# The first two rows of query weights multiplied with the two token tiles one by one

## The chip, the cores and the metric

The kernel runs on one core of one Trainium2 chip. The metric is the device time of one execution in microseconds (us). TensorE is called PE here, its weight loads PEld, VectorE DVE, ScalarE ACT, GpSimd POOL; SP issues DMAs.

## The reference

The program is an encoder trunk of two layers over 256 tokens of width 1024. Each layer has a mixer (retention, a linear recurrence and attention side by side, with one input and one output projection) and then a PEER channel mixer. The PEER part, cut to what matters here:

```python
def peer(x, wq, keys, u, v):          # x: the tokens after RMSNorm
    q = (xt @ wq).reshape(T, PEER_HEADS, 2, PEER_HALF)     # 256 x 1024 @ 1024 x 2048
    s = jnp.einsum('thpk,hpnk->thpn', q, keys, ...)
    sv, si = lax.top_k(s, PEER_TOPK)
    ...
    # gather 16 experts per head and token, gelu, weighted sum
```

## The kernel before

Tokens are held transposed: `hT` and `lT` are 128 x 8 x 256, that is eight blocks `d` of 128 channels by 256 tokens. `hT` is the value rounded to the matmul's 4-byte format, `lT` the rest that the rounding took away. Each weight tile is split the same way into `hi` (ACT, line 140) and `lo` (DVE or POOL, line 141). A product is then made of three matmuls (`three`, lines 205 to 207): hi with hT, hi with lT, lo with hT. The weights are the stationary operand, 128 x 128, and the tokens are the moving operand, 256 columns at a time. Every matmul has a weight load of its own ahead of it.

The tokens come as two tiles of 128 rows. At the end of the mixer the output projection (`wout`) is done for token tile 0, then `norm_T` normalises that tile, transposes it on PE (line 197), and writes its 128 columns of `hT` (ACT, line 201) and `lT` (DVE, line 202). The same follows for tile 1. While DVE, POOL and ACT normalise tile 1, PE has no more output projection to do.

`peer` begins with the query projection. Its loop runs over four blocks `b` of 512 query columns, and in each over four weight tiles `d2`; one weight tile has two rows `k` of 128 channels and four groups `c` of 128 columns, so 2 x 4 x 3 = 24 matmuls of 256 columns. The results gather in two PSUM banks `pq`. After the last `d2`, ACT copies them out (line 719), and PE makes the scores with the keys (line 723). The four raw tiles and four hi/lo pairs are rotating buffers. Splits of block 0 go to DVE for even `d2` and to POOL for odd ones.

A scheduler, not the order of the code alone, sets the order in which each engine gets its instructions; within an engine they run in that order, and one that waits holds up all behind it.

Of the kernel before, what the change touches and what calls it, by code (L numbers as in the profile page):

```python
# [18 lines left out]
P = 128  # L19
D = 1024  # L20
T = 256
NT = 2
DEPTH = 2
EPS = 1e-6
ND = D // P
# [84 lines left out]
def trunk(ctx, tc, x, rows, lru_col, lru_gw, w_in, w_out, ln2_w, peer_wq, peer_kt, peer_ut, peer_v, lnf_w,  # L110
# [9 lines left out]
    def acc_tile():  # L120
        return ps.tile([P, 512], F32, tag="acc", bufs=4, name="acc")
# [4 lines left out]
    def hd_tile():  # L126
        return ps.tile([P, 512], F32, tag="hd", bufs=2, name="hd")

    def raw_tile():
        return sp.tile([P, D], F32, tag="raw", bufs=RAW, name="raw")  # L130

    def hl_tiles():
        return (sp.tile([P, D], F32R, tag="hi", bufs=HL, name="hi"),
                sp.tile([P, D], F32R, tag="lo", bufs=HL, name="lo"))

    def eng(pattern, a):
        return G if pattern[a % len(pattern)] == "G" else V

    def split(src, hi, lo, lo_eng=None):
        A.activation(hi, src, AF.Copy)  # L140
        (lo_eng or V).tensor_sub(lo, src, hi.bitcast(F32))  # L141
# [62 lines left out]
    def three(o, lh, ll, rh, rl, first, last, skip=False):  # L204
        TE.matmul(o, lh, rh, start=first, stop=False, skip_group_check=skip)  # L205
        TE.matmul(o, lh, rl, start=False, stop=False, skip_group_check=skip)  # L206
        TE.matmul(o, ll, rh, start=False, stop=last, skip_group_check=skip)  # L207

    hT = cp.tile([P, ND, T], F32R, name="hT")
    lT = cp.tile([P, ND, T], F32R, name="lT")  # L210
# [389 lines left out]
    def peer(l, pp):  # L600
# [100 lines left out]
        for b in range(4):  # L701
            pq = [acc_tile() for _ in range(2)]
            for d2 in range(4):
                raw = raw_tile()
                nc.sync.dma_start(raw.rearrange("p (k c) -> p k c", k=2),
                                  peer_wq[l, d2 * 2 * P:(d2 + 1) * 2 * P, b * 512:(b + 1) * 512]
                                  .rearrange("(k p) c -> p k c", p=P))
                hi, lo = hl_tiles()
                split(raw, hi, lo, eng(WP0 if b == 0 else WP1, d2))
                for k in range(2):  # L710
                    d = d2 * 2 + k
                    for c in range(4):
                        s = slice(k * 512 + c * P, k * 512 + (c + 1) * P)
                        o = pq[c // 2][:, (c % 2) * T:(c % 2 + 1) * T]
                        first, last = d == 0 and c % 2 == 0, d == ND - 1
                        three(o, hi[:, s], lo[:, s], hT[:, d], lT[:, d], first, last, skip=True)
                sa.adv(2.4)
            for c in range(2):
                A.activation(qs[:, 2 * c:2 * c + 2], pq[c].rearrange("p (k t) -> p k t", k=2), AF.Copy)
            for tt in (1, 0):  # L720
                pt = hd_tile()
                for k in range(4):
                    TE.matmul(pt[:, k * NK:(k + 1) * NK], qs[:, k, tt * P:(tt + 1) * P], keyT[:, b * 4 + k],
                              start=k == 0, stop=True, skip_group_check=True)
                A.activation(scs[:, tt, b * 4:b * 4 + 4], pt.rearrange("p (k n) -> p k n", k=4), AF.Copy)  # L725
            sa.add(topk(1, b))
# [146 lines left out]
    for l in range(layers):  # L873
        with tc.tile_pool(name=f"mp{l}", bufs=1) as mp, tc.tile_pool(name=f"ms{l}", bufs=2) as ms:
            mix(l, mp, ms)
        if do_peer:
            with tc.tile_pool(name=f"pp{l}", bufs=1) as pp:
                peer(l, pp)
# [50 lines left out]
```

## Time and profile before

| | us |
|---|---|
| median of 3 runs | 1975.18 (1974.17 to 1978.27) |
| the profiled execution | 1973.99 |
| its span, first to last instruction | 1972.2 |
| PE busy in it | 1881.7 (95%) |
| mean granted PE clock | 0.979 |

A row of a timeline gives the start in us from the span's start, the duration, engine, line, operation, output and inputs, and how many instructions were merged in the row; in brackets stands the idle time of the engine before it and what ended that. Durations of pipelined matmuls overlap, so the pace of a run of them is read from the distance between starts. Of the two levels of the PE clock, 1.2 and 2.4 GHz, a granted clock of 0.50 is the lower and 1.00 the upper.

### The profile page before, as it was taken

What the parts mean: (1) busy time and instruction counts of PE and PEld (TensorE: products, weight loads), DVE (VectorE), ACT (ScalarE), POOL (GpSimd) and SP (SyncE); (2) the same over time, 40 slices, a digit from 0 to 9 for tenths busy, and PEclk for the clock granted to TensorE, in tenths of its full rate; (3) what the DMA queues carried; (4) which work ended last, traced back from release to release, by engine and by line L of the source; (5) the groups of instructions that cost most, each with busy time, mean ns of one, the idle gap of its engine ahead of it and who ended that gap; (6) DMA issues with size and microseconds to landing.
All of it is one profiled execution on the core that took longest, in us unless ns stands there. A gap on an engine that the chain in (4) does not pass through costs nothing. (4 is left out here: it accounts for less than half of the span.)

```text
span 1972.2 us, 34047 instructions
## 1 busy us (share of the span) xinstructions
PE 1881.7 (95%) x13348; PEld 1662.5 (84%) x13348; DVE 1512.7 (77%) x2716; ACT 901.0 (46%) x1378; POOL 563.3 (29%) x238
## 2 busy tenths in 40 slices
PE   6888999999999999999978889999999999999998
PEld 5658999999999877788866689999999998777886
DVE  6965999789855699755569569995997557996555
ACT  4444544444444443444454344445434444434443
POOL 3615788200000134100056168881000002440000
PEclk9988999999999999999988899999999999999999
DMA  5405555545555544555454055555445555446553
GB/s 185 145 25 182 162 190 183 192 154 163 166 183 192 171 139 161 185 189 191 151 164 132 23 198 170 184 185 191 151 160 172 189 186 171 150 142 201 185 189 128
DMA packets 95280, 324.41 MB, mean 164 GB/s; under 512 B 10128, under 2 KB 10640, under 8 KB 94864
## 3 DMA queue, kind: packets, MB, share of 16 engines
q1 hardware_dynamic: 92384, 314.61, 49.0%
q10 hardware_dynamic: 2736, 7.63, 1.1%
q8 instruction: 104, 1.70, 0.3%
q14 instruction: 56, 0.46, 0.1%
HBM read 321.16 MB, written 1.05 MB: 163 GB/s over the span
## 5 line engine op out<-in xcount | busy, mean ns | idle before, releaser
L140 ACT ACTIVATE hi<-raw 128x1024 fp32r<-128x1024 f32 (+1 forms) x600 | 627.3, 1047 | 529.2 <-issue 176.9
L141 POOL TENSOR_TENSOR lo<-raw,hi 128x1024 fp32r<-128x1024 f32 (+1 forms) x202 | 530.4, 2633 | 919.8 <-ACT hi L140 900.1
L141 DVE TENSOR_TENSOR lo<-raw,hi 128x1024 fp32r<-128x1024 f32 x398 | 491.6, 1236 | 201.9 <-ACT hi L140 201.9
L205 PE MATMUL acc<-hi,ph 128*128 128x512 f32 x1024 | 410.2, 401 | 0.0
L207 PE MATMUL acc<-hi,pl 128*128 128x512 f32 x1024 | 404.8, 396 | 0.4 <-DVE pl L141 0.4
L206 PE MATMUL acc<-lo,ph 128*128 128x512 f32 x1024 | 404.9, 395 | 0.0
L205 PE MATMUL tr<-hT,hi 128*128 128x256 f32 x1024 | 290.8, 284 | 0.0
L205 PE MATMUL hd<-hT,hi 128*128 128x256 f32 x1024 | 290.5, 284 | 0.0
L140 ACT ACTIVATE ph<-Gt 128x256 fp32r<-128x256 f32 x256 | 106.4, 417 | 400.6 <-PE acc L206 389.6
L206 PE MATMUL hd<-lT,hi 128*128 128x256 f32 x1024 | 287.8, 281 | 0.0
L206 PE MATMUL tr<-lT,hi 128*128 128x256 f32 x1024 | 287.6, 281 | 0.0
L207 PE MATMUL hd<-hT,lo 128*128 128x256 f32 x1024 | 287.5, 281 | 0.0
L207 PE MATMUL tr<-hT,lo 128*128 128x256 f32 x1024 | 287.5, 281 | 0.0
L207 PEld LDWEIGHTS acc<-hi,pl 128*128 128x128 f32 x1024 | 192.4, 188 | 48.2 <-DVE pl L141 2.4
L206 PEld LDWEIGHTS acc<-lo,ph 128*128 128x128 f32 x1024 | 192.9, 188 | 41.4
L205 PEld LDWEIGHTS acc<-hi,ph 128*128 128x128 f32 x1024 | 192.7, 188 | 41.3 <-ACT ph L140 0.5
L141 DVE TENSOR_TENSOR pl<-Gt,ph 128x256 fp32r<-128x256 f32 x256 | 124.6, 489 | 127.7 <-ACT ph L140 127.7
L205 PEld LDWEIGHTS hd<-hT,hi 128*128 128x128 f32 x1024 | 193.1, 189 | 1.5 <-ACT Gt L725 0.4
L205 PEld LDWEIGHTS tr<-hT,hi 128*128 128x128 f32 x1024 | 193.1, 189 | 1.1
L206 PEld LDWEIGHTS tr<-lT,hi 128*128 128x128 f32 x1024 | 193.0, 188 | 1.0
L206 PEld LDWEIGHTS hd<-lT,hi 128*128 128x128 f32 x1024 | 193.0, 188 | 0.9
L207 PEld LDWEIGHTS hd<-hT,lo 128*128 128x128 f32 x1024 | 192.9, 188 | 0.0
(204 smaller groups left out, 2622.6 us busy)
## 6 DMA issues: line engine op xcount, KB each, us to landing
raw<-in_peer_ut_dram SPq DMA_DIRECT2D x256, 512.0 KB, 3.4
raw<-in_peer_v_dram SPq DMA_DIRECT2D x256, 512.0 KB, 4.2
raw<-in_peer_wq_dram SPq DMA_DIRECT2D x32, 512.0 KB, 3.8
raw<-in_w_in_dram SPq DMA_DIRECT2D x24, 512.0 KB, 3.6
raw<-in_w_out_dram SPq DMA_DIRECT2D x16, 512.0 KB, 3.4
raw<-in_w_in_dram SPq DMA_DIRECT2D x16, 384.0 KB, 3.4
Gt<-in_peer_kt_dram ACTq DMA_DIRECT2D x2, 1024.0 KB, 6.1
row<-in_rows_dram ACTq DMA_DIRECT2D x4, 256.0 KB, 4.9
```

Source lines behind the costliest of these rows:

```text
L140: A.activation(hi, src, AF.Copy)
L141: (lo_eng or V).tensor_sub(lo, src, hi.bitcast(F32))
L205: TE.matmul(o, lh, rh, start=first, stop=False, skip_group_check=skip)
L206: TE.matmul(o, lh, rl, start=False, stop=False, skip_group_check=skip)
L207: TE.matmul(o, ll, rh, start=False, stop=last, skip_group_check=skip)
```

## The change

For the first weight tile of the first block (`b == 0 and d2 == 0`) the 24 matmuls of 256 columns become two passes of 24 matmuls of 128 columns: first token tile 0, then token tile 1. Everything else keeps its code. In both layers this makes 48 matmuls, each with its weight load, out of 24.

```diff
-                for k in range(2):
-                    d = d2 * 2 + k
-                    for c in range(4):
-                        s = slice(k * 512 + c * P, k * 512 + (c + 1) * P)
-                        o = pq[c // 2][:, (c % 2) * T:(c % 2 + 1) * T]
-                        first, last = d == 0 and c % 2 == 0, d == ND - 1
-                        three(o, hi[:, s], lo[:, s], hT[:, d], lT[:, d], first, last, skip=True)
+
+                parts = [slice(tt * P, (tt + 1) * P) for tt in range(NT)] if b == 0 and d2 == 0 else [slice(0, T)]
+                for t in parts:
+                    for k in range(2):
+                        d = d2 * 2 + k
+                        for c in range(4):
+                            s = slice(k * 512 + c * P, k * 512 + (c + 1) * P)
+                            o = pq[c // 2][:, (c % 2) * T + t.start:(c % 2) * T + t.stop]
+                            first, last = d == 0 and c % 2 == 0 and t.start == 0, d == ND - 1
+                            three(o, hi[:, s], lo[:, s], hT[:, d, t], lT[:, d, t], first, last, skip=True)
```

The order of the instructions on DVE, ACT, POOL and SP is the same in both programs. On PE it differs at two places, one in each layer. The first is in layer 0, PE's queue at the end of the output projection; `tr` is the PSUM tile of the transposes of token tile 1, `hi_1250` and `lo_1251` are the first query weight tile, `acc_1246` and `acc_1247` the two banks `pq`. Before:

```order
L197 MATMUL tr_1221<-ident_71,raw_1208 128x128 [waits DVE_49,PE_49]
L197 MATMUL tr_1221<-ident_71,raw_1208 128x128 x3
L197 MATMUL tr_1229<-ident_71,raw_1208 128x128 [waits DVE_49,PE_49]
L197 MATMUL tr_1229<-ident_71,raw_1208 128x128 x3
L205 MATMUL acc_1246<-hT_75,hi_1250 128x256 [waits Activation_49]
L205 MATMUL acc_1247<-hT_75,hi_1250 128x256
L206 MATMUL acc_1246<-lT_76,hi_1250 128x256 [waits DVE_49]
L207 MATMUL acc_1246<-hT_75,lo_1251 128x256
```

And the same place now:

```order
L205 MATMUL acc_1246<-hT_75,hi_1250 128x128 [waits Activation_49]
L197 MATMUL tr_1221<-ident_71,raw_1208 128x128 [waits DVE_49,PE_49]
L197 MATMUL tr_1221<-ident_71,raw_1208 128x128 x3
L197 MATMUL tr_1229<-ident_71,raw_1208 128x128 [waits DVE_49,PE_49]
L197 MATMUL tr_1229<-ident_71,raw_1208 128x128 x3
L206 MATMUL acc_1246<-lT_76,hi_1250 128x128
L207 MATMUL acc_1246<-hT_75,lo_1251 128x128 [waits DVE_49]
L205 MATMUL acc_1246<-hT_75,hi_1250 128x128
```

One matmul of token tile 0 stands ahead of the transposes of tile 1; the other 47 stand behind them, and the first wait on DVE after the transposes is now on `lo` (line 141) and not on `lT` (line 202).

The passage from token tile 0 to tile 1, PE in layer 0, now:

```order
L205 MATMUL acc_1247<-hT_75,hi_1250 128x128
L206 MATMUL acc_1247<-lT_76,hi_1250 128x128
L207 MATMUL acc_1247<-hT_75,lo_1251 128x128
L205 MATMUL acc_1246<-hT_75,hi_1250 128x128 [waits Activation_49]
L206 MATMUL acc_1246<-lT_76,hi_1250 128x128 [waits DVE_49]
```

The waits for tile 1's `hT` and `lT` have moved here, 24 matmuls further back. In layer 1 PE's queue differs in the same way, one matmul ahead of the eight transposes and 47 behind them.

## Rows read from the trace of the kernel before

**Rows 1.** The page, first part: busy us, share and instructions of each engine.
```profile
PE 1881.7 (95%) x13348; PEld 1662.5 (84%) x13348; DVE 1512.7 (77%) x2716; ACT 901.0 (46%) x1378; POOL 563.3 (29%) x238
```
**Rows 2.** Timeline of PE, layer 0, end of output projection and first query weights.
```profile
157.21 0.39 PE L207 MATMUL acc<-hi,mixL 128*128 128x512 f32 x1
161.53 1.94 PE L197 MATMUL tr<-ident,raw 128*128 128x128 f32 x8 [3.93 <-DVE raw L188]
163.30 0.79 PE L205 MATMUL acc<-hT,hi 128*128 128x256 f32 x2
165.73 0.58 PE L206 MATMUL acc<-lT,hi 128*128 128x256 f32 x1 [1.63 <-DVE lT L202]
166.11 0.41 PE L207 MATMUL acc<-hT,lo 128*128 128x256 f32 x1
...
169.95 0.32 PE L205 MATMUL acc<-hT,hi 128*128 128x256 f32 x1
170.11 0.28 PE L206 MATMUL acc<-lT,hi 128*128 128x256 f32 x1
...
170.35 0.28 PE L205 MATMUL acc<-hT,hi 128*128 128x256 f32 x1
```
**Rows 3.** Timelines of DVE and ACT, same stretch, and DVE's next row behind it.
```profile
161.69 3.38 DVE L141 TENSOR_TENSOR lo<-raw,hi 128x1024 fp32r<-128x1024 f32 x1
165.00 1.27 DVE L202 TENSOR_TENSOR lT<-tr,hT 128x512 fp32r<-128x512 f32 x2
...
181.99 0.30 DVE L635 MAX8 Gt<-Gt 128x8 f32<-128x128 f32 x1 [14.58 <-ACT Gt L725]
...
159.51 1.99 ACT L140 ACTIVATE hi<-raw 128x1024 fp32r<-128x1024 f32 x2
```
**Rows 4.** Timeline of PE, the same place in layer 1.
```profile
1138.44 1.06 PE L197 MATMUL tr<-ident,raw 128*128 128x128 f32 x8 [3.93 <-DVE raw L188]
...
1142.63 0.58 PE L206 MATMUL acc<-lT,hi 128*128 128x256 f32 x1 [2.09 <-DVE lT L202]
1143.01 0.41 PE L207 MATMUL acc<-hT,lo 128*128 128x256 f32 x1
...
1146.00 0.39 PE L207 MATMUL acc<-hT,lo 128*128 128x256 f32 x1
...
1146.94 0.28 PE L205 MATMUL acc<-hT,hi 128*128 128x256 f32 x1
```
**Rows 5.** Timelines of DVE and ACT in layer 1.
```profile
1138.61 3.37 DVE L141 TENSOR_TENSOR lo<-raw,hi 128x1024 fp32r<-128x1024 f32 x1
...
1136.42 1.99 ACT L140 ACTIVATE hi<-raw 128x1024 fp32r<-128x1024 f32 x2
```
**Rows 6.** Weight loads of lines 478 and 207: duration ns min/median/max, first and last start.
```profile
L478 PEld LDWEIGHTS hd<-pT,vt x64: 132/136/231, 119.6 to 1107.1; 128*64 128x64 f32 x64
L207 PEld LDWEIGHTS acc<-hT,lo x320: 186/188/333, 16.8 to 1195.5; 128*128 128x128 f32 x160
```
**Rows 7.** Timeline of PE, the scores of block 0, and the line's instruction count.
```profile
179.01 1.16 PE L723 MATMUL hd<-Gt 128*128 128x128 f32 x8
179.92 0.37 PE L205 MATMUL acc<-hT,hi 128*128 128x256 f32 x1
...
L723 PE MATMUL hd<-Gt x128: 270/275/377, 179.0 to 1198.4; 128*128 128x128 f32 x128
```
**Rows 8.** Busy us by engine, PE clock granted, DMA share and GB/s, by stretch.
```profile
166.00:170.00 4.00, 4.00 (x20) 4.00 (x21) 1.41 (x2) 0.39 (x1) 0.00 (x0) 0.50 0.86 254
170.00:174.00 4.00, 4.00 (x35) 4.00 (x35) 0.00 (x0) 2.42 (x3) 3.25 (x2) 1.00 0.72 277
...
112.00:116.00 4.00, 4.00 (x12) 2.41 (x11) 2.62 (x9) 2.28 (x8) 0.00 (x0) 0.50 0.00 0
...
200.00:210.00 10.00, 9.96 (x85) 9.76 (x84) 9.93 (x36) 5.34 (x7) 8.05 (x4) 1.00 0.51 158
```
**Rows 9.** Timeline of PE in the stretch of layer 0 from 111.5.
```profile
111.54 3.66 PE L446 MATMUL hd<-kT,qT 64*128 64x256 f32 x8 [0.85 <-ACT pr L457]
```

## The prediction

> **What bounds the kernel now.** I read the page first: PE is recorded busy for 95% of the span [rows 1], so a change on PE counts wherever the others keep up. Then I read PE's timeline where the change sits. After the last matmul of the output projection at 157.21 PE waits 3.93 us for DVE to normalise token tile 1, transposes it from 161.53, runs two query matmuls at 163.30, and waits again, 1.63 us, until DVE has written `lT` [rows 2]. From 165.73 on it runs without a gap. DVE's own timeline says why `lT` is late: the 3.38 us `lo` of the first weight tile stands ahead of it and ends at 161.69 + 3.38 = 165.07; the first half of `lT` follows [rows 3]. Layer 1 is the same: 3.93 us, then 2.09 us until 1142.63, with `lo` ending at 1138.61 + 3.37 = 1141.98 [rows 4, 5]. The idle time is what the change could fill. Behind this place PE has no slack (9.96 of 10 us busy in a later stretch [rows 8]), and DVE's next instruction waits 14.58 us for scores that PE makes [rows 3]. So a shift of PE here goes to the end in full.
>
> **What the order allows.** Only one of the 48 matmuls stands ahead of the transposes. It needs the first of two ACT splits, done near 159.51 + 1.0 = 160.5 in layer 0 and 1137.4 in layer 1 [rows 3, 5], and so it falls into the idle time before 161.53 and 1138.44: cost nothing, covered by 1.0 us. If the split came later than that, the transposes, `hT` and `lT` queued behind it would be late by as much. Behind the transposes one more matmul has its data; the next waits for `lo`. The 3.93 us wait is therefore not filled at all. What is won is that PE goes on when `lo` is ready and not half an `lT` later: 165.73 - 165.12 = 0.61 us in layer 0 and 1142.63 - 1142.03 = 0.60 in layer 1 (0.05 us allowed from the end of `lo` to PE). Tile 1's `hT` and `lT`, now needed 22 matmuls later, are long done then. No DMA moves; the orders of DVE, ACT, POOL and SP are unchanged, and a later PE only gives the weight tiles more time.
>
> **What 128 columns cost.** No matmul of 128 columns in this format is in the trace, so I bound it. The pace at 256 columns is 0.213 us at 1.2 GHz (166.11 to 169.95 in 18 steps) and 0.118 at 2.4 GHz [rows 2]. If only the moving columns counted, half of that would do: 0.107 and about 0.06. But each matmul loads 128 columns of 4-byte weights. The loads of 64 such columns take 132 to 136 ns and those of 128 take 186 to 188; at the lower clock the maxima are 231 and 333 [rows 6]. So 64 columns more cost 52 ns at the upper and 102 ns at the lower level, and 128 columns stream for 104 to 108 ns and about 205 to 213: as long as the 256 moving columns do. Loads cannot be quicker than that one after another, so I take the old pace for the new matmul: 0.213 us low, and high the 0.113 us at which 128-column f32 passes with such loads follow each other ((179.92 - 179.01) / 8) [rows 7]. The split then halves no time and doubles the count.
>
> The Trainium skill ("TensorE: Matmul & The Clock Gate", LDWEIGHTS) puts a weight load at its columns divided by 1.2, in ns, whatever the clock: 107 ns for 128. The trace agrees at the upper level and not at the lower, where loads take longer [rows 6]; by that rule the lower-level pace would be 0.107 and the change would come out as the second rival below. The same page (Back-to-back issue gap) gives about 81 ns for load and matmul pairs of 128 columns at full clock; no row here shows that, and by it the first rival would come to about 1978.
>
> **The sum if the clock stays low.** In layer 0 the third matmul starts at 165.12; the restart took 0.38 us before [rows 2], so the fourth starts at 165.50, and the 49th (the first of the next weight tile) 45 x 0.2133 = 9.60 us later, at 175.10. Before, that tile began with the 25th at 170.35 [rows 2]: 4.75 us lost. In layer 1: 1142.03 + 0.38 + 9.60 = 1152.01 against 1146.94 [rows 4]: 5.07 us lost. Together 9.8.
>
> Does the clock stay low? Before, it rose 4.2 us (169.95) and 3.5 us (1146.1) after PE began to run without gaps [rows 2, 4, 8]. Recorded busyness is not what raises it: from 112 to 116 PE shows 4.00 of 4 us busy at a granted 0.50 [rows 8], in matmuls that use 64 of the 128 rows [rows 9]. A stretch in which the array waits half of its time for weights looks to me more like that one than like the dense one, so I expect 1.2 GHz through the whole split. Then the clock comes back some time within the next tile. Between no delay and the 4.2 us seen before, 0 to 20 matmuls run at 0.213 instead of 0.118: 0 to 1.9 us a layer; I take 1.0. The total is 9.8 + 2.0 = +11.8 us, bounds +9.8 and +13.6. On the profiled 1973.99 that is 1985.8; the median of the runs lies 1.19 above that execution, so **1987.0**.
>
> **The rivals.**
> 1. *Weight loads bind, but the clock rises when it did before.* For it: PE has work without a gap. Layer 0: 165.50 to 169.95 holds 20.9 steps, the 49th comes 24 x 0.113 after 169.98, at 172.7, +2.35. Layer 1: 17.2 steps to 1146.1, then 27 x 0.113 and one mixed step, 1149.3, +2.4. Sum +4.75: 1979.9; a rise 0.6 us earlier in each layer would take 0.6 off.
> 2. *Not slower: the loads hide and 128 columns cost half.* The place is the same 46 matmuls, the price 0.107 at the low level. Layer 0: 165.50 + 45 x 0.1067 = 170.30 against 170.35; layer 1: 1147.2, or 1146.75 with the rise at 1146.1, against 1146.94. Sum within 0.3 us of nothing, 1975.2. It decides from the point where a 128-column load streams in under about 0.11 us at 1.2 GHz; the 333 against 231 ns speak against. Even a free second pass could give back no more than the 0.61 + 0.60 us of the earlier start, so no case here is faster by 0.2%.
> 3. *Short matmuls lose the format's single pass.* Plain f32 of 128 columns runs as two passes (64 matmuls issued on line 723 leave 128 records [rows 7]), 0.226 us high and about 0.43 low. With the rise where it was, the 49th comes 7.4 us late in each layer: 1990; with the clock low throughout, 14.7 each: 2005. Against it: at 256 and 512 columns this format keeps one record for each matmul.
>
> **How the numbers follow.** Chances: the forecast 0.52; rival 1 0.25; rival 2 0.13; rival 3 0.10, mostly near 1990. 0.2% is 3.95 us, about what a measurement of this kernel can tell from no change. Rival 2 is "same" and so is the low edge of rival 1 (a quarter of it, 0.06): 0.19. The rest is slower, less 0.01 for disturbances that end faster. The range runs from rival 1 (1979) over the forecast's bounds (1985.0 to 1988.8) to rival 3 with the rise (1991); it leaves out rival 2 and the far end of rival 3, some 0.17.
>
> **What would show it.** In the changed kernel's PE timeline: one 128-column matmul ahead of the transposes at about 160.6 and 1137.5; the restart at about 165.1 and 1142.0, released by DVE's `lo`, not `lT`; the starts of the 46 that follow 0.213 us apart (0.107 would make rival 2, 0.43 rival 3); granted clock 0.50 up to about 175 and 1152 (1.00 from 170 and 1146 would make rival 1); the scores of block 0 at about 184.8 instead of 179.01. What would make me wrong on the large scale is a load that overlaps another load, or a clock that counts the loads as work.

## The result, and the profile after the change

The changed kernel takes 1990.14 us (median of 6 runs, 1986.58 to 1995.85) against 1975.03 for the kernel before (6 runs, 1971.20 to 1978.27): a ratio of 1.0076, 95% interval 1.0063 to 1.0089. It is 15.1 us slower. The forecast was 1987.0 with a range of 1979 to 1991. The profiled execution took 1990.49 us with a span of 1988.6, that is 16.4 more than the 1972.2 before.

The page's first part answers to [rows 1]: 48 matmuls more, 15.9 us more of busy PE, and hardly a change on the other engines.

```profile
PE 1897.6 (95%) x13396; PEld 1679.4 (84%) x13396; DVE 1515.6 (76%) x2716; ACT 900.5 (45%) x1378; POOL 568.1 (29%) x238
```

PE's timeline of the changed kernel in layer 0 answers to [rows 2] and the first row of [rows 7]; columns: start, duration of the row's instructions, engine, line, operation, operands, count, and in brackets the idle time ahead and its releaser. The scores, line 723 before, are L726 here.

```profile
160.25 0.48 PE L205 MATMUL acc<-hT,hi 128*128 128x128 f32 x1 [3.00 <-ACT hi L140]
161.18 1.94 PE L197 MATMUL tr<-ident,raw 128*128 128x128 f32 x8 [0.46 <-DVE raw L188]
...
164.78 0.47 PE L207 MATMUL acc<-hT,lo 128*128 128x128 f32 x1 [1.55 <-DVE lo L141]
165.05 0.41 PE L205 MATMUL acc<-hT,hi 128*128 128x128 f32 x1
165.27 0.41 PE L206 MATMUL acc<-lT,hi 128*128 128x128 f32 x1
...
174.44 0.41 PE L207 MATMUL acc<-hT,lo 128*128 128x128 f32 x1
174.65 0.52 PE L205 MATMUL acc<-hT,hi 128*128 128x256 f32 x1
...
179.67 0.32 PE L207 MATMUL acc<-hT,lo 128*128 128x256 f32 x1
...
185.65 1.16 PE L726 MATMUL hd<-Gt 128*128 128x128 f32 x8
```

Three things are to be seen. One matmul stands in the former wait and fills 0.48 us of it. PE restarts at 164.78, released by `lo`. And from 165.27 to 174.44 there are 43 steps in 9.17 us, 0.213 us each: the step that 256 columns had at the lower clock, now paid for half the columns.

The windows of the changed kernel answer to the first two of [rows 8]; columns: the stretch, its length, busy us and count of PE, PEld, DVE, ACT and POOL, the granted clock, DMA share and GB/s.

```profile
166.00:170.00 4.00, 4.00 (x21) 4.00 (x20) 1.06 (x1) 0.55 (x1) 0.00 (x0) 0.50 0.92 285
170.00:174.00 4.00, 4.00 (x20) 4.00 (x20) 0.00 (x0) 0.50 (x1) 2.35 (x1) 0.50 0.63 237
...
178.00:182.00 4.00, 4.00 (x29) 4.00 (x29) 0.00 (x0) 1.06 (x1) 1.09 (x2) 0.78 0.40 131
```

The granted clock stays at 0.50 (1.2 GHz) all through the split and for 5 us of the next weight tile; before, it was 1.00 from 170 on. Layer 1 repeats it:

```profile
1147.43 1.94 PE L197 MATMUL tr<-ident,raw 128*128 128x128 f32 x8 [0.45 <-DVE raw L188]
...
1151.03 0.47 PE L207 MATMUL acc<-hT,lo 128*128 128x128 f32 x1 [1.54 <-DVE lo L141]
...
1160.90 0.52 PE L205 MATMUL acc<-hT,hi 128*128 128x256 f32 x1
...
1166.12 0.31 PE L205 MATMUL acc<-hT,hi 128*128 128x256 f32 x1
...
1171.97 1.16 PE L726 MATMUL hd<-Gt 128*128 128x128 f32 x8
```

**Where the 16.4 us come from.** I compare rows of the two profiles that do the same work. Ahead of layer 0's place the changed kernel is 0.34 early (the start of its `lo` on DVE, 161.35 against 161.69). The first 256-column matmul of the next weight tile starts at 174.65 against 170.35 [rows 2]: 4.64 lost with that offset. From there to the scores of block 0 it takes 11.00 us instead of 8.66 (170.35 to 179.01 [rows 2, 7]): 2.34. The kernel is then 6.64 behind. At the transposes of layer 1 it is 1147.43 - 1138.44 = 8.99 behind: 2.35 were lost in work that the change does not touch. In layer 1 the next tile starts at 1160.90 against 1146.94 [rows 4]: 4.97 lost; to the scores 11.07 us instead of 8.66 (they stood at 1155.60): 2.41. Sum: -0.34 + 4.64 + 2.34 + 2.35 + 4.97 + 2.41 = 16.37.

The 2.35 us between the two places lie in the mixer of layer 1. Up to some 1046 us before, stretches of the two kernels shifted by 6.64 have nearly the same PE time and clock; further on the stretches at half clock fall elsewhere, as these two windows show, the first of the kernel before and the second of the changed one:

```profile
1080.00:1100.00 20.00, 16.70 (x52) 9.81 (x52) 16.14 (x45) 10.74 (x34) 2.34 (x1) 0.66 0.17 53
```
```profile
1086.64:1106.64 20.00, 16.88 (x47) 9.71 (x46) 16.71 (x44) 10.18 (x32) 3.17 (x2) 0.61 0.17 53
```

Measured in the same way against the same profile of the kernel before, this stretch cost -0.2 to +4.7 us in the profiles of the experiments below, and in the kernel that came out fastest among them +1.7. With the changed kernel's it is positive in seven of eight profiles, so it looks as if the one execution it is measured against was quick there. I count it as scatter and as no part of the change; that it has nothing to do with it was not shown on its own.

### The profile page after: what moved, and what is told of

Read it like the earlier page. It is cut to its first block, busy times and chain, and to the rows that moved or that the text cites. A ratio compares the mean times of both kernels' runs of the same rounds, so it can differ in the third digit from the quotient of the medians.

```text
span 1988.6 us, 34143 instructions
## 1 busy us (share of the span) xinstructions
PE 1897.6 (95%) x13396; PEld 1679.4 (84%) x13396; DVE 1515.6 (76%) x2716; ACT 900.5 (45%) x1378; POOL 568.1 (29%) x238
```

## The experiments

All kernels are measured against the kernel before on the same chip. Two of them, the ones with narrower weight loads, ran once; they have no interval, and what follows from them is read from the profile.

**Does the weight load set the pace?** The theory of the forecast: at the lower clock a 128-column load of 4-byte weights takes 0.213 us, and the 128 moving columns hide behind it. The rival: something that goes with each matmul, or with its moving columns, sets the step. The experiment halves the loads of the split's second row, which leaves out that row's share of half the query columns, and leaves the moving columns alone:

```
-  s = slice(k * 512 + c * P, k * 512 + (c + 1) * P)
-  o = pq[c // 2][:, ...]
+  n = 64 if b == 0 and d2 == 0 and k else P
+  s = slice(k * 512 + c * P, k * 512 + c * P + n)
+  o = pq[c // 2][:n, ...]
```

> As the changed kernel, but in the split weight tile the second row (k = 1) loads only the first 64 of each 128 weight columns, so the upper 64 query columns of each group lack that row's share (that work is left out). The 48 matmuls of 128 token columns alternate: 12 with 128-column loads, 12 with 64-column loads, twice. Theory W (the weight load binds): at 1.2 GHz the wide ones start 0.213 us apart, the narrow ones 0.107; the split takes about 7.7 us instead of 10.2 in each layer, the first 256-column matmul starts near 172.1 instead of 174.65. Rival C (128 columns in this format take as long as 256 by themselves, the loads hide): 0.213 us for all 48, no change against the changed kernel.

It took 1984.29 us in one run (before: 1978.1). PE's timeline across the border of the two rows, and the weight loads there (PEld):

```profile
167.16 0.41 PE L206 MATMUL acc<-lT,hi 128*128 128x128 f32 x1
167.37 0.41 PE L207 MATMUL acc<-hT,lo 128*128 128x128 f32 x1
167.59 0.31 PE L205 MATMUL acc<-hT,hi 128*64 128x128 f32 x1
167.69 0.31 PE L206 MATMUL acc<-lT,hi 128*64 128x128 f32 x1
...
172.71 0.52 PE L205 MATMUL acc<-hT,hi 128*128 128x256 f32 x1
```
```profile
167.27 0.33 PEld L207 LDWEIGHTS acc<-hT,lo 128*128 128x128 f32 x1
167.48 0.23 PEld L205 LDWEIGHTS acc<-hT,hi 128*64 128x64 f32 x1
```

At the same clock and with the same 128 moving columns the step is 0.213 us with 128 weight columns (168.87 to 171.43 in 12 steps) and 0.107 with 64 (167.59 to 168.87 in 12). The load sets the pace, and the rival falls. Writing 128 output rows instead of 64 is not the reason either: 256 columns of them are written in the same 0.213 us [rows 2]. The Trainium skill ("TensorE: Matmul & The Clock Gate", LDWEIGHTS) gives a load its columns divided by 1.2, in ns, and names no clock level: 107 ns for 128 columns. For these 4-byte weights the trace disagrees at the lower level, where 128 columns take 213 ns.

**Do 128-column matmuls pull the clock down, or only fail to raise it?** The split is moved to block 1, where PE comes from dense work and runs at 2.4 GHz:

```
-  parts = [...] if b == 0 and d2 == 0 else [slice(0, T)]
+  parts = [...] if b == 1 and d2 == 0 else [slice(0, T)]
```

> The same split, moved from block 0 to block 1, first weight tile, where PE runs without a gap at 2.4 GHz; block 0 is as before. Theory K1 (the half-waiting matmuls do not hold the clock up): the first of the 48 start 0.113 us apart, the granted clock falls to 0.50 during or just after the split, and the cost in each layer is 24 x 0.113 = 2.7 us plus 1 to 5 us at the lower level: total +8 to +15 over before, 1983 to 1990. Rival K2 (they count as work like any other): the clock stays at 1.00, total +5.4, 1980. Rival C at the upper level: 0.118 us each or more, not distinguishable from W here.

The ratio is 1.0019 (1.0006 to 1.0031), +3.7 us. PE's timeline (a 128-column matmul early in the split, then its end) and a window inside it:

```profile
182.09 0.27 PE L206 MATMUL acc<-lT,hi 128*128 128x128 f32 x1
...
186.89 0.27 PE L207 MATMUL acc<-hT,lo 128*128 128x128 f32 x1
187.00 0.33 PE L205 MATMUL acc<-hT,hi 128*128 128x256 f32 x1
```
```profile
184.00:186.00 2.00, 2.00 (x21) 2.00 (x20) 2.00 (x16) 0.00 (x0) 0.00 (x0) 1.00 0.72 240
```

The granted clock holds at 1.00 through the split, whose matmuls are 0.112 us apart (182.09 to 187.00 in 44 steps). So the same instructions keep the upper level where PE has it, and did not bring it back in the 9.9 us of the changed kernel. Rival K2 of the expectation came, and theory K1 with its 1983 to 1990 fails. At the upper level the split costs about 24 x 0.112 = 2.7 us a layer, two of which lie within the interval of the timed difference (1.2 to 6.1 us); from the scores of block 0 to those of block 1 it is 16.32 us (179.45 to 195.77) instead of 13.45 (179.01 to 192.46), +2.9.

**Is the cost in proportion?** Only the first of the two rows is split:

```
-  for t in parts:
-      for k in range(2):
-          d = d2 * 2 + k
+  split0 = b == 0 and d2 == 0
+  for k in range(2):
+      d = d2 * 2 + k
+      parts = [...] if split0 and k == 0 else [slice(0, T)]
+      for t in parts:
```

> Only the first of the two rows is split: 24 matmuls of 128 columns, then 12 of 256. If the cost is a count of slots of 0.213 us plus a late clock: 12 added slots, 2.56 us, less 0.6 for the earlier start, so the second weight tile starts near 172.3 (170.35 before, 174.65 in the changed kernel) and the clock rises 3 to 5 us after the last 128-column matmul, about 173 to 175; total +5 to +9, 1980 to 1984. If the clock is not held back by 128-column work, it rises near 170 as before, and the total is +3 at most, 1978.

The ratio is 1.0010 (1.0000 to 1.0019): +2 us, with 0 to 3.8 in the interval. PE's timeline:

```profile
164.00 0.47 PE L207 MATMUL acc<-hT,lo 128*128 128x128 f32 x1 [1.55 <-DVE lo L141]
...
168.75 0.52 PE L205 MATMUL acc<-hT,hi 128*128 128x256 f32 x1
...
172.68 0.28 PE L205 MATMUL acc<-hT,hi 128*128 128x256 f32 x1
```

The clock comes up 3.9 us after the first 256-column matmul and 8.7 after the restart, again not within the 128-column ones. Compared row by row as above, the two places cost 2.8 and 3.1 us in this profile, 5.9 together and within the +5 to +9 that were expected; the timed difference lies below that, so the expectation missed the time. The difference between the profile and the timing is not settled: the profile of the kernel before is one execution, at the lower end of the 25 timed beside this one (1973.99 against a median of 1978.1).

**What keeps the clock low: the short matmul, or the wait for its weights?** All split matmuls but the four that open a PSUM bank get 64-column loads, so that 128 moving columns (0.107 us) and the load (0.107) last equally long:

```
+  first, last = d == 0 and c % 2 == 0 and t.start == 0, d == ND - 1
+  n = 64 if b == 0 and d2 == 0 and not first else P
+  s = slice(k * 512 + c * P, k * 512 + c * P + n)
+  o = pq[c // 2][:n, ...]
```

> The changed kernel with 64-column weight loads for all matmuls of the split weight tile but the four that open a PSUM bank; the upper 64 query columns of each group lack these rows' share (left out). If the pace is the weight load's, the 46 matmuls behind the wait start 0.107 us apart and the split ends about 4.9 us after the wait, near 170. If waiting for weights is what kept the clock low, these matmuls, which stream without a wait, bring the granted clock up within 5 us of their start, near 170 or soon after it; if the length of the moving operand (128 columns) is what keeps it low, the rise comes 3.3 to 5.2 us after the first 256-column matmul as in the changed kernel, 173 to 175.

One run, 1977.24 us, against a median of 1975.75 before. PE's timeline and a window:

```profile
164.41 0.47 PE L207 MATMUL acc<-hT,lo 128*128 128x128 f32 x1 [1.55 <-DVE lo L141]
...
165.75 0.31 PE L206 MATMUL acc<-lT,hi 128*64 128x128 f32 x1
165.85 0.31 PE L207 MATMUL acc<-hT,lo 128*64 128x128 f32 x1
...
169.67 0.22 PE L207 MATMUL acc<-hT,lo 128*64 128x128 f32 x1
169.73 0.33 PE L205 MATMUL acc<-hT,hi 128*128 128x256 f32 x1
...
1149.31 0.22 PE L205 MATMUL acc<-hT,hi 128*64 128x128 f32 x1
```
```profile
170.00:174.00 4.00, 4.00 (x36) 4.00 (x35) 0.00 (x0) 2.21 (x3) 3.76 (x2) 1.00 0.56 198
```

The clock rises inside the split: in layer 0 5.2 us after the restart, at the last matmuls of the split, and in layer 1 4.0 us after it (1145.23 to 1149.24), with 12 of them still to come, which then follow 0.06 us apart. The two places cost +0.2 and -0.1 us. This is what the second rival of the forecast promised for a load that hides. That the matmuls have 128 columns is not what kept the clock low: with the same columns and twice the load behind each it did not rise in 9.9 us. The narrower loads change more than one thing, however: the wait for weights is gone, the matmuls come twice as often, and half of the array's columns stay unused. These were not separated, and why the chip treats the two kernels differently stays open.

**Can the 3.93 us wait be filled?** The order lets one matmul into it, since `lo` is made behind the normalisation of tile 1. Here the first query weight tile is loaded and split (ACT, DVE) ahead of that normalisation:

```
+  if tt:
+      raw = raw_tile()
+      nc.sync.dma_start(raw..., peer_wq[l, 0:2 * P, 0:512]...)
+      q0[:] = hl_tiles()
+      split(raw, *q0, V)
```

> The changed kernel with the first query weight tile loaded and split (ACT, DVE) ahead of the normalisation of token tile 1, so that all 24 matmuls of token tile 0 stand ahead of the transposes of tile 1 and fill PE's wait. DVE's lo (1.2 us) delays that normalisation by about 1.1 us. If 128 columns cost 0.113 us at 2.4 GHz and the clock stays up through the short wait that is left: tile 0 from 158 to 160.8, transposes near 162.5, tile 1 to about 167.5, second weight tile 2.8 us earlier than before in each layer, total -5.7, 1969. If the clock falls all the same (theory K1), tile 1 runs at 0.213: 169.8, gain 0.5 less a late rise of up to 2 us: total -1 to +4, 1974 to 1979.

The ratio is 1.0011 (1.0002 to 1.0021), +2.2 us against the kernel before: about 13 of the 15 lost are won back, and no gain is left. PE's timeline, and that of DVE and POOL:

```profile
157.55 0.22 PE L205 MATMUL acc<-hT,hi 128*128 128x128 f32 x1
...
160.51 0.27 PE L207 MATMUL acc<-hT,lo 128*128 128x128 f32 x1
...
164.23 1.94 PE L197 MATMUL tr<-ident,raw 128*128 128x128 f32 x8 [3.45 <-DVE raw L188]
...
171.48 0.52 PE L205 MATMUL acc<-hT,hi 128*128 128x256 f32 x1
```
```profile
161.53 2.95 DVE L188 TENSOR_SCALAR raw<-raw,nrs 128x512 f32<-128x512 f32 x2 [0.45 <-POOL nrs L183]
```
```profile
161.47 2.34 POOL L141 TENSOR_TENSOR lo<-raw,hi 128x1024 fp32r<-128x1024 f32 x1
```

The 24 matmuls of token tile 0 now run from 157.55 at the upper clock. But the wait has moved and not gone: 3.45 us after them, for DVE's two normalising instructions, which take 2.95 us where they took 0.88. They start 0.06 us after POOL's `lo` of the second weight tile. The clock falls in that wait, and tile 1 is done at the lower level, as in the second case of the expectation.

**Is POOL's `lo` the cause?** The same kernel with the split of the second weight tile held back behind tile 1's `hT` and `lT`; `later()` is the kernel's own helper that issues what stands under it behind marked instructions:

```
-  split(raw, hi, lo, eng(WP0 if b == 0 else WP1, d2))
+  with later() if b == 0 and d2 == 1 else ExitStack():
+      split(raw, hi, lo, eng(WP0 if b == 0 else WP1, d2))
```

> The run with the early first weight tile (e7_early_split), and the second weight tile's split (ACT and POOL) held back behind the transposes' hT and lT of token tile 1. There, POOL's lo ran beside DVE's scaling of the rows (L188), which then took 2.95 us instead of 0.88; that should fall to 0.9 and the transposes come 2.1 us earlier, near 162.2. Then tile 1 and the second weight tile start 2 us earlier in each layer than in that run: 2 x 2 us, ratio to before 0.998 to 1.000. If DVE's slow row has another cause, nothing moves and the ratio stays at 1.001.

The ratio is 1.0006 (0.9995 to 1.0017): no difference that can be told. DVE's, then PE's timeline (the last two rows are layer 1):

```profile
161.80 0.88 DVE L188 TENSOR_SCALAR raw<-raw,nrs 128x512 f32<-128x512 f32 x2 [0.45 <-POOL nrs L183]
```
```profile
162.43 1.06 PE L197 MATMUL tr<-ident,raw 128*128 128x128 f32 x8 [1.37 <-DVE raw L188]
164.47 0.33 PE L206 MATMUL acc<-lT,hi 128*128 128x128 f32 x1 [0.29 <-DVE lT L202]
...
167.11 0.52 PE L205 MATMUL acc<-hT,hi 128*128 128x256 f32 x1
...
1141.71 1.06 PE L197 MATMUL tr<-ident,raw 128*128 128x128 f32 x8 [1.37 <-DVE raw L188]
...
1148.50 0.52 PE L205 MATMUL acc<-hT,hi 128*128 128x256 f32 x1
```

DVE is back at 0.88 us and the wait is down from 3.45 to 1.37, as expected, so POOL's `lo` was the cause; the gain in time that was expected with it does not show. In layer 0 nearly all 24 matmuls of tile 1 run at the upper clock, and the first 256-column matmul starts at 167.11, 3.2 us earlier than the one in its place before [rows 2]; the clock falls at about 166.8 all the same, until about 170.2, and the place gains 2.0 us. In layer 1 the wait is 1.37 us as well, but the clock falls just behind the transposes, near 1143.0: tile 1 runs at 0.213 us a matmul, the clock is back only at 1153.3, and the place loses 1.0 us. With the wait filled so far, the split gains nothing that can be measured, and what it comes to hangs on where the clock falls.

**The same step without the split.** The last kernel is the kernel before with that one edit, the held-back split of the second weight tile:

> The kernel before, without any splitting of columns, with the second weight tile's split held back behind token tile 1's hT and lT. If DVE's 3.38 us lo (L141) is long because POOL's lo runs beside it, it falls to 1.2 us, lT is ready about 1.6 us earlier and PE restarts near 164.0 instead of 165.7 in each layer; the clock comes up the same time after that or at most 1.6 us later. Total -1.5 to -3.5 us, ratio 0.998 to 0.999. If not, the ratio is 1.000.

The ratio is 0.9977 (0.9966 to 0.9989), by which it is 4.5 us faster than the kernel before in the 17 runs beside it; the medians differ by 2.9 (1972.87 against 1975.75). It is the only kernel here that is faster than the one before, and by the ratio by a little more than was expected. DVE's and PE's timelines:

```profile
161.87 1.22 DVE L141 TENSOR_TENSOR lo<-raw,hi 128x1024 fp32r<-128x1024 f32 x1
```
```profile
161.70 1.94 PE L197 MATMUL tr<-ident,raw 128*128 128x128 f32 x8 [3.93 <-DVE raw L188]
164.20 0.58 PE L206 MATMUL acc<-lT,hi 128*128 128x256 f32 x1
...
167.14 0.29 PE L205 MATMUL acc<-hT,hi 128*128 128x256 f32 x1
...
176.88 1.16 PE L724 MATMUL hd<-Gt 128*128 128x128 f32 x8
```

The 3.93 us wait is untouched. The 3.38 us `lo` that stood ahead of `lT` [rows 3] takes 1.22, PE goes on at 164.20 instead of 165.73, and the clock is up at 167.14 instead of 169.95. The two places give 2.3 and 2.0 us. The next `lo` on DVE now takes 2.62 us beside POOL's held-back one, but PE does not wait for it.

## Why the prediction was right, step by step

1. **What the order allows** was right. One matmul stood ahead of the transposes (160.25, forecast about 160.6), the 3.93 us were not filled, and PE went on when `lo` was ready: 161.35 + 3.38 = 164.73, restart 164.78 in layer 0, and the same in layer 1.
2. **The weight load as the price of 128 columns** was right, and the half-load kernel shows it. The 0.213 us were measured to the third digit; the 0.113 taken for the upper level is 0.112 in the block-1 kernel. The second rival (the loads hide) falls, and so does the third (two passes): there is one record for each matmul and no step near 0.43.
3. **The split's own cost** was 4.64 and 4.97 us against 4.75 and 5.07. The difference is the restart, which took 0.27 us and not 0.38.
4. **The clock stays low through the split**: right, so that the first rival falls. The reason given, that a stretch that waits for weights looks more like the half-used stretch at 112 us than like the dense one, was only a likeness. The kernel with all loads narrow bears it out as far as it goes: without that wait the clock rose. And the likeness has a limit: in block 1 the same matmuls kept the upper level, a case that the forecast did not ask about.
5. **The tail was the term that was mis-sized.** It was put at 0 to 1.9 us a layer and taken as 1.0; it measured 2.34 and 2.41, beyond its upper bound. The bound assumed that the clock would be back at most 4.2 us after the next tile's first matmul, the longest delay seen before. It took 5.1 us (174.65 to 179.7) and 5.2 (1160.90 to 1166.1), some 24 matmuls at 0.213 instead of 0.118 us, which is 2.3 us. Two delays from one execution were treated as a limit. The block-1 kernel, whose block 0 is the old code, took 4.9 and 4.4 us from its restart to the rise, so the limit did not hold even there; after a first 256-column matmul the experiments add 2.9 to 4.8 us.
6. **The sum**: 11.8 forecast, 14.4 measured at the two places (9.6 split, 4.7 tail), 15.1 in the medians. Of the profile's 16.4, another 2.35 are the mixer stretch. The time lies above the forecast's own upper bound, 1988.8, and inside the range only because its end, 1991, stood there for the third rival, which did not happen. That it was still inside is luck; the mechanism and the size of the split's own cost are not.

The forecast also took the 3.38 us `lo` as it stood. It was the thing worth asking about: its neighbour of the same shape, the next `lo` on DVE in the kernel before, takes 1.21 us, and the experiment that mended it is the only kernel that gained.

```profile
166.20 1.21 DVE L141 TENSOR_TENSOR lo<-raw,hi 128x1024 fp32r<-128x1024 f32 x1
```

## What to carry over

Before a matmul is cut along its moving columns, compare the weight load with the columns that are left: below the load's own time the cut halves nothing and doubles the count. An order that is meant to fill a wait has to be checked for what the moved work itself waits for; here one matmul of 48 was free to move. And where an instruction takes far longer than its like, look at what runs beside it on the other engines, before rearranging those that wait for it.

## What the runs showed of the hardware

**The clock depends on where it starts.** The 48 matmuls with 128-column loads and 128 moving columns stayed at 0.50 for 9.9 us in the changed kernel and at 1.00 for the whole of the split in block 1. A fall of the clock therefore costs more ahead of load-bound work than ahead of dense work: in layer 0 it rose 4.2 us after the restart before, 2.9 with the earlier `lo`, and only 14.9 us (164.78 to 179.7) after it with the split. Nor does the wait ahead settle it in these runs: behind the 1.37 us wait of the early kernel with the held-back split the clock fell after 4.4 us in layer 0 (162.43 to 166.8) and after 1.3 in layer 1 (1141.71 to 1143.0).

**VectorE and GpSimd get in each other's way.** In the kernel before POOL works on its `lo` from 161.62 to 163.99:

```profile
161.62 2.37 POOL L141 TENSOR_TENSOR lo<-raw,hi 128x1024 fp32r<-128x1024 f32 x1 [0.76 <-ACT hi L140]
```

DVE's `lo`, begun at 161.69, ends at 165.07 [rows 3]. Alone it takes 1.22 us, and 163.99 + 1.22 = 165.21: within 0.14 us of a DVE that stands still until POOL is done. The early-split kernel repeats it with two other instructions: POOL ends at 161.47 + 2.34 = 163.81, and 163.81 + 0.88 = 164.69, where DVE's 161.53 + 2.95 = 164.48. The Trainium skill ("SBUF — State Buffer", Who interferes with whom) states that a VectorE instruction with two SBUF inputs, or one in a two-port mode, and a GpSimd instruction that reads SBUF exclude each other, the second to come waiting until the first is done. These rows agree to 0.2 us; that the scaling (L188) runs in such a mode is not shown by them.
